# A two-layer trunk with streamed fp32 weights: second SwiGLUs that begin with a whole pair of blocks, and three smaller moves

## The chip, the cores and the metric

The kernel runs on one core of one Trainium2 chip. The metric is the device time of one launch in microseconds; lower is better. The names of the engines: PE is TensorE (matrix products), DVE is VectorE, ACT is ScalarE, POOL is GpSimd, SP is SyncE, which here issues the loads of weights. Each engine works off its own list of instructions in order and stops at the first one whose semaphore is not there yet.

## The reference

The input is 512 tokens of width 1024. Two layers, each of four stages, and a final RMSNorm:

```python
for i in range(DEPTH):                                     # DEPTH = 2
    h = h + 0.5 * swiglu(rmsnorm(h, ffn1_norm[i]), ffn1_w_gu[i], ffn1_w_down[i])
    u = rmsnorm(h, mix_norm[i])                            # the mixer: gated convolution + attention, 8 heads
    ...
    h = h + merged @ w_o[i]
    h = h + 0.5 * swiglu(rmsnorm(h, ffn2_norm[i]), ffn2_w_gu[i], ffn2_w_down[i])
    gate = jax.nn.sigmoid(rmsnorm(h, ple_norm[i]) @ w_ple_gate[i])
    h = h + gate * (p[i] @ w_ple_proj[i])
return rmsnorm(h, final_norm)

def swiglu(x, w_gu, w_down):
    g, u = jnp.split(x @ w_gu, 2, axis=-1)                 # D_FF = 2816 columns each
    return (jax.nn.silu(g) * u) @ w_down
```

All data are fp32, and the result has to be as good as fp32.

## The kernel before, in words

**Names.** The four stages of the layers 0 and 1 are called `a0`, `a1` (first SwiGLU), `m0`, `m1` (mixer), `b0`, `b1` (second SwiGLU), `e0`, `e1` (the gate with the per-layer input). Tiles begin with the stage's name: `b0x` is a normalised input of `b0`, `b00b` the PSUM tile "b" of quad 0 of `b0`, `a02d` the tile "d" of quad 2 of `a0`.

**Numbers.** A product in fp32 is three matmuls: an operand is split into a high part that PE takes at full rate and a low part (the rest), and `mm3` (lines 279 to 281) adds high·high, high·low and low·high. Activations lie with their 1024 features in 8 tiles of 128 partitions by 512 tokens (`h`), so a matmul of full width streams 512 columns.

**Weights.** SP loads them in pieces of 128 x 1024 (512 KB) into 10 buffers `st`. ACT makes the high part `wh` (line 71), DVE the rest `wl` (line 72), in 4 buffers each. Whatever PE does next thus has three things behind it: the load, ACT's cast and DVE's subtraction. Lines 150 to 168 (DVE) make sums and differences of weight pieces.

**A SwiGLU.** The 2816 columns of gate and up make 22 blocks of 128, in 11 pairs. A pair is done in one of two ways. *Whole*: 96 matmuls of 512 columns (8 tiles of features, gate and up of both blocks, three matmuls each). *By seven products*, a Strassen-Winograd scheme over blocks, halves of the features and halves of the tokens: the class `Quad` makes the combinations of weights, the class `Halved` those of the activations (`row(j)`: tiles `x`, `t`, `y`, `u`, lines 480 to 499 and their splits, once for each of four feature tiles), and `Sevens` has the steps. Its steps are numbered by product: 1, 2, 6 and 4 are *joint* ones (lines 545 and 549: 8 matmuls of 512 columns and 8 of 256), and 5, 7 and 3 are full ones (line 559: 24 of 256 columns) or joint, depending on the form. A step can begin with a *seed*: ACT copies a PSUM tile into another (line 565, 128 x 1024), and the next products are added to the copy. Each output goes through `finish` (lines 637 to 642: times 1/rms, Silu, gate times up). The down projection (`down`) runs beside later quads: a `pd` tile is seeded by ACT with twice the residual (line 680), the products are added to it, and ACT writes half of it back to `h` (line 684).

**What sets the order.** The program is written in the order in which PE is to work. Within that the framework's scheduler decides where ACT's and DVE's work stands in their lists; `tc.issue_after(x)` holds a piece behind an instruction.

**The normalisation.** `normed` makes the 8 inputs `x` of a stage from `h` without waiting for 1/rms; the sum of squares `acc` goes through a ones matmul (`ps`, lines 357 and 358), `rms` makes 1/rms (`r`, lines 361 to 365) from it, and `r` is multiplied in afterwards (`activate` for a whole block, lines 671 to 680, `finish` for the others).

**PSUM.** It has 8 banks of 128 x 512 fp32. `banks.paired()` shares them out as two double tiles "chain" (`PB`, banks 0 to 3), one double tile "seeded" (`PA`, banks 4 and 5) and two single ones (`PS`, banks 6 and 7). `banks.eight()` makes 8 single ones, for the attention and for the last stage `e1`.

**The four SwiGLUs differ in how they begin.** `a0` does its first 4 blocks (2 pairs) whole; `a1` its first 2 blocks (one pair), and two of the four `Halved` rows are made while the inputs come in. `b0` and `b1` do none whole: quads 0 and 1 are interleaved by hand, with special forms of `Quad` and `Sevens` ("early"), pieces of the token sums split one by one, and chains of `issue_after`.

**The mixer** ends its input projections with such quads too (`m1g3a`, `b`, `d`). Then come, for the first pair of heads, keys `kn0`, queries `qn0`, keys `kn1`, queries `qn1` and values `v0`, `v2`, each in a PSUM tile that must be split by ACT (line 271) and DVE (line 272) before the bank is used again.

Of the kernel before, what the change touches and what calls it, by code (L numbers as in the profile page):

```python
# [9 lines left out]
F32 = mybir.dt.float32  # L10
# [3 lines left out]
ALU = mybir.AluOpType  # L14
AX = mybir.AxisListType

P = 128
# [16 lines left out]
class Stream:  # L34
# [27 lines left out]
    def split(self, src, step=1024):  # L62
# [3 lines left out]
        for c in range(0, 1024, step):  # L66
            w = slice(c, c + step)
            if i == c == 0:
                self.nc.vector.tensor_copy(hi[:, w], src[:, w])
            else:  # L70
                self.nc.scalar.copy(hi[:, w], src[:, w])  # L71
            last = self.nc.vector.tensor_tensor(lo[:, w], src[:, w], hi[:, w].bitcast(F32), ALU.subtract)  # L72
        self.last_split = last.ins
# [57 lines left out]
class Quad:  # L131


    def __init__(self, W, quarters, early):
        self.W, self.early = W, early
        for q in ("a11", "a21", "a22", "a12"):
            setattr(self, q, W.raw(quarters[q]))

    def part(self, j):
# [12 lines left out]
        if self.early:  # L152
            if j == 5:
                self.s = W.buffer("s")
                tt(self.s, self.a21, self.a22, ALU.add)
                return W.split(self.s)
            if j == 6:
                tt(self.s, self.s, self.a11, ALU.subtract)  # L158
                return W.split(self.s)
            tt(self.a11, self.a11, self.a21, ALU.subtract)  # L160
            return W.split(self.a11)
# [32 lines left out]
def trunk_kernel(ctx, tc, dims, x, p, positions, gains, rope_c, final_row, weights, out):  # L194
# [263 lines left out]
    class Halved:  # L458
# [16 lines left out]
        def own(self, j, xs, parts=False):  # L475
# [7 lines left out]
            if parts:  # L483
                split_to(th[:, left], tl[:, left], t[:, left])
            self.ys[1].append(self.both(xs[j], left))
            self.ys[5].append((th[:, left], tl[:, left]))
            self.half[j] = x, t, th, tl, parts

        def other(self, j, xs):
# [4 lines left out]
            x, t, th, tl, parts = self.half.pop(j)  # L494
            y, u = G(f"{self.name}y{j}"), G(f"{self.name}u{j}")
            x_ins = nc.scalar.mul(y, h[k], gain(self.nm, self.l, k))
# [3 lines left out]
            at = right if parts else slice(0, S)  # L500
            split_to(th[:, at], tl[:, at], t[:, at])
# [3 lines left out]
            for p_, at in ((6, left), (4, right)):  # L505
                v = G(f"{self.name}u{j}_{p_}", F32R).rearrange("p (a t) -> p a t", t=H)
                last = split_to(v[:, 0, :], v[:, 1, :], u[:, at])
                self.ys[p_].append((v[:, 0, :], v))
            return x_ins.ins, last.ins

    class Sevens:
# [7 lines left out]
        def __init__(self, w, l, name, ys, columns, done, early=0):  # L519
            self.w, self.l, self.name, self.ys, self.columns, self.done, self.early = w, l, name, ys, columns, done, early  # L520
            self.todo = {}

        def quad(self, n):
            if n not in self.todo:
# [3 lines left out]
                self.todo[n] = {"w": Quad(W, quarters, n < self.early)}  # L528
            return self.todo[n]

        def split(self, n, j):

            d = self.quad(n)
            d["part", j] = d["w"].part(j)
# [4 lines left out]
        def joint(self, ps, d, j):  # L539

            hi, lo = d.pop(("part", j), None) or d["w"].part(j)
# [9 lines left out]
        def product(self, ps, d, j, start=False):  # L551

            hi, lo = d.pop(("part", j), None) or d["w"].part(j)
            for k, v in enumerate(self.ys[j]):
                vh, vl = v if j in (5, 7) else (v[0], v[1][:, 1, :])
                for w in range(2):
                    at = slice((2 * k + w) * P, (2 * k + w + 1) * P)
                    for i, (a_, b_) in enumerate(((hi, vh), (hi, vl), (lo, vh))):
                        nc.tensor.matmul(ps[:, w, :], a_[:, at], b_, start=start and w + k + i == 0,
                                         stop=k == 3 and i == 2, skip_group_check=True)  # L560
# [12 lines left out]
        def step(self, n, j):  # L573
            d, H, early = self.quad(n), self.H, n < self.early
            tt = nc.vector.tensor_tensor
            if j == 1:
                d["b"] = PB(f"{self.name}{n}b")
                self.joint(d["b"], d, j)
                if not early:
                    self.seed(n, "a")  # L580
            elif j == 2:
                self.joint(d["a"], d, j)
                self.out(n, d.pop("a"), 0, 0)
                if n + 1 < self.early:
                    self.seed(n + 1, "a")
            elif j == 6:
                self.joint(d["b"], d, j)
                if early:
                    d["u"] = [self.tile(n, f"u{w}") for w in range(2)]
                    for w in range(2):  # L590
                        nc.scalar.copy(d["u"][w], d["b"][:, :, w * H:(w + 1) * H])
                    tt(d["c5"], d["c5"], d["u"][1], ALU.add)
                else:
                    self.seed(n, "d")
            elif j == 5:
                d["c5"] = self.tile(n, "c5")
                if early:
                    d["c"] = PS(f"{self.name}{n}c").rearrange("p (w t) -> p w t", t=H)
                    self.product(d["c"], d, j, True)
                    nc.scalar.copy(d["c5"], d["c"])  # L600
                else:
                    self.product(d["d"][:, :, H:], d, j)
                    nc.scalar.copy(d["c5"], d["d"][:, :, H:])
            elif j == 7:
                self.product(d["b"][:, :, :H], d, j)
                t = d.pop("c5")
                tt(t, d["b"][:, :, :H], t, ALU.add)
                self.done(n, 1, 1, t, t)
            elif j == 3 and early:
                self.product(d["c"], d, j)  # L610
                t, l = d.pop("u")
                tt(t, t, l, ALU.add)
                tt(t, d.pop("c"), t, ALU.add)
                self.done(n, 0, 1, t, t)
# [7 lines left out]
    def ffn(l, nm, name, first=False, beside=iter(()), early=2):  # L622
# [6 lines left out]
        n_whole = 4 if first else 0 if early > 2 else 2  # L629
# [3 lines left out]
        def finish(n, f, c, src, t):  # L633
# [9 lines left out]
            if whole:  # L643
# [3 lines left out]
                        finish, 0 if n_whole else 2)  # L647
        step = sevens.step

        def early_rows(k, xs):  # L650

            j = k - KD // 2
            if n_whole == 0:
                if j < 0:
                    ys.own(k, xs, True)
                elif j < early:
                    ys.other(j, xs)
# [679 lines left out]
```

## Time and profile before

| | us |
|---|---|
| median of 3 runs (2284.45 to 2286.79) | 2286.35 |
| the profiled execution | 2286.7 |
| its span, first to last instruction | 2284.9 |
| PE busy | 2254.5 (99%), 12272 matmuls |
| DVE busy | 1746.8 (76%) |
| ACT busy | 1447.3 (63%) |
| DMA queue of the weights | 28.6% of 16 engines |

The span begins with the first instruction and ends with the last; 1.8 us of the profiled execution lie around it. A matmul's row gives its own duration (389 ns for 512 columns), but they are pipelined: the next one starts some 0.23 us after it. What a stretch of PE costs is therefore read from starts. PE is idle for 30 us in all, and the time is this idle time, what the clock gate takes, and the matmuls' own pace.

### The profile page before, as it was taken

The page shows a single profiled execution, that of the slowest core. Times are in us where ns is not written, and L with a number is a line of the kernel's source. Part 1 is how long each engine was busy: PE and PEld are TensorE (multiplying, and loading weights), DVE is VectorE, ACT ScalarE, POOL GpSimd, SP SyncE. Part 2 cuts the span into 40 slices and gives each one's busy share as a digit, 9 for nine tenths or more (in the row PEclk, how much of TensorE's full clock was granted, in tenths as well). Part 3 has the DMA queues.
Part 4 walks back from the last instruction along what each step waited for, and adds up shares of the span by engine and source line. Part 5 has one row for each costly group of instructions (what it writes and reads, how often), then busy time and mean ns, then how long its engine had stood idle before and what let it go on. Part 6 is the DMA issues. An engine that isn't in the chain of part 4 may idle for free.

```text
span 2284.9 us, 31443 instructions
## 1 busy us (share of the span) xinstructions
PE 2254.5 (99%) x12272; PEld 1959.8 (86%) x12272; DVE 1746.8 (76%) x2465; ACT 1447.3 (63%) x2250; POOL 40.4 (2%) x42
## 2 busy tenths in 40 slices
PE   9899999999999999999999999999999999999998
PEld 7788888888888888888888888888888888888887
DVE  7787766887877987776797777668878679777756
ACT  6666666456654666666676666655567466666664
POOL 0000000000210000000000000000002000000000
PEclk9999999999999999999999999999999999999999
DMA  5233232133121233324223333332221213332321
GB/s 213 87 103 105 99 132 99 65 102 102 47 93 65 84 120 102 111 96 146 83 78 107 102 102 111 111 102 83 93 74 65 102 37 125 107 111 101 111 94 37
DMA packets 63364, 223.07 MB, mean 98 GB/s; under 512 B 7280, under 2 KB 7280, under 8 KB 63216
## 3 DMA queue, kind: packets, MB, share of 16 engines
q1 hardware_dynamic: 62640, 220.28, 28.6%
q8 instruction: 96, 1.57, 0.3%
q10 hardware_dynamic: 576, 0.79, 0.1%
q14 instruction: 52, 0.43, 0.1%
HBM read 218.94 MB, written 2.10 MB: 97 GB/s over the span
## 4 chain that ended last, share of the span: by engine, by line
PE 93%; DVE 4%; ACT 2%; issue 0%; DMA 0%; SPq 0%; ACTq 0%; DVEq 0%
PE a1pd L279 2%; PE b1pd L279 2%; PE b0pd L279 2%; PE b1pd L280 2%; PE a1pd L280 2%; PE b0pd L280 2%; PE a0pd L279 2%; PE b0pd L281 2%; PE a1pd L281 2%; PE b1pd L281 2%; PE a0pd L280 2%; PE a0pd L281 2%; DVE wl L72 1%; ACT wh L71 1%; PE m0mop L279 1%; PE m1mop L279 1%
## 5 line engine op out<-in xcount | busy, mean ns | idle before, releaser
L72 DVE TENSOR_TENSOR wl<-st,wh 128x1024 fp32r<-128x1024 f32 (+1 forms) x504 | 610.6, 1213 | 320.4 <-ACT wh L71 318.7
L71 ACT CAST wh<-st 128x1024 fp32r<-128x1024 f32 (+1 forms) x503 | 523.4, 1044 | 414.7 <-PE b1pd L280 13.4
L72 DVE TENSOR_TENSOR wl<-s,wh 128x1024 fp32r<-128x1024 f32 x53 | 64.6, 1220 | 1.0 <-ACT wh L71 1.0
L71 ACT CAST wh<-s 128x1024 fp32r<-128x1024 f32 x53 | 55.1, 1040 | 12.8 <-DVE s L158 4.5
L150 DVE TENSOR_TENSOR st<-st,s 128x1024 f32<-128x1024 f32 x49 | 59.8, 1220 | 0.0
L163 DVE TENSOR_TENSOR st<-st,st 128x1024 f32<-128x1024 f32 x45 | 55.1, 1224 | 1.3
L165 DVE TENSOR_TENSOR s<-st,st 128x1024 f32<-128x1024 f32 x45 | 54.9, 1219 | 0.1
L168 DVE TENSOR_TENSOR st<-st,st 128x1024 f32<-128x1024 f32 x45 | 54.8, 1217 | 0.0
L684 ACT ACTIVATE h<-a0pd 128x512 f32<-128x512 f32 x41 | 24.3, 597 | 23.1 <-PE a0pd L281 23.0
L684 ACT ACTIVATE h<-b1pd 128x512 f32<-128x512 f32 x41 | 24.4, 597 | 21.6 <-PE b1pd L281 21.6
L684 ACT ACTIVATE h<-b0pd 128x512 f32<-128x512 f32 x41 | 24.4, 597 | 21.1 <-PE b0pd L281 21.0
L684 ACT ACTIVATE h<-a1pd 128x512 f32<-128x512 f32 x41 | 24.2, 597 | 19.0 <-PE a1pd L281 18.7
L680 ACT ACTIVATE b1pd<-h 128x512 f32<-128x512 f32 x41 | 24.6, 602 | 3.5 <-DVE b110o L570 1.4
L680 ACT ACTIVATE b0pd<-h 128x512 f32<-128x512 f32 x41 | 24.6, 602 | 3.5 <-DVE b010o L570 1.4
L680 ACT ACTIVATE a0pd<-h 128x512 f32<-128x512 f32 x41 | 24.5, 601 | 2.5 <-DVE a010o L570 1.7
L680 ACT ACTIVATE a1pd<-h 128x512 f32<-128x512 f32 x41 | 24.5, 601 | 2.2 <-DVE a110o L570 1.4
L108 POOL MEMSET wh<- 128x256 f32 x4 | 1.1, 312 | 1194.0 <-DVE wl L72 1194.0
L280 PE MATMUL a0p<-a0x,wh 128*128 128x512 f32 x44 | 17.2, 392 | 0.0
L281 PE MATMUL a0p<-a0x,wl 128*128 128x512 f32 x44 | 17.1, 389 | 0.0
L279 PE MATMUL a0p<-a0x,wh 128*128 128x512 f32 x44 | 17.1, 389 | 0.0
L274 ACT ACTIVATE b0x<-h,cols 128x512 fp32r<-128x512 f32 x8 | 5.8, 726 | 14.3 <-DVE h L1087 14.2
L274 ACT ACTIVATE b1x<-h,cols 128x512 fp32r<-128x512 f32 x8 | 5.8, 724 | 14.3 <-DVE h L1087 14.2
(6607 smaller groups left out, 7588.8 us busy)
## 6 DMA issues: line engine op xcount, KB each, us to landing
st<-in_weights SPq DMA_DIRECT2D x406, 512.0 KB, 3.3
h<-in_x SPq DMA_DIRECT2D x8, 256.0 KB, 5.4
st<-in_weights SPq DMA_DIRECT2D x7, 256.0 KB, 5.3
out<-e1d SPq DMA_DIRECT2D x4, 256.0 KB, 2.1
out<-fh SPq DMA_DIRECT2D x3, 256.0 KB, 2.2
e0pi<-in_p SPq DMA_DIRECT2D x2, 256.0 KB, 4.0
e1pi<-in_p SPq DMA_DIRECT2D x2, 256.0 KB, 3.8
fg<-in_final_row SPq DMA_DIRECT2D x2, 256.0 KB, 4.8
```

The source lines that it names most:

```text
L71: self.nc.scalar.copy(hi[:, w], src[:, w])
L72: last = self.nc.vector.tensor_tensor(lo[:, w], src[:, w], hi[:, w].bitcast(F32), ALU.subtract)
L150: tt(self.a12, self.a12, self.s, ALU.subtract)
L163: tt(self.a11, self.a11, self.a21, ALU.subtract)
L165: tt(self.s, self.a22, self.a11, ALU.subtract)
L168: tt(self.a21, self.a21, self.a22, ALU.add)
L274: nc.scalar.activation(hi, src, AF.Copy, scale=scale)
L279: nc.tensor.matmul(ps, wh, vh, start=first, stop=False, skip_group_check=seeded)
L280: nc.tensor.matmul(ps, wh, vl, start=False, stop=False, skip_group_check=seeded)
L281: nc.tensor.matmul(ps, wl, vh, start=False, stop=last, skip_group_check=seeded)
L680: nc.scalar.mul(ps, h[m], 2.0)
L684: nc.scalar.mul(h[m], ps, 0.5)
```

## The change

It has five parts.

1. **Second SwiGLUs (`b0`, `b1`).** They get the code of `a1`: the first pair of blocks is done whole, two of the `Halved` rows are made while the inputs come in, and the sevens begin with quad 1. All the code of the interleaved beginning is deleted. The keyword `early` now means the number of rows made ahead: 2 for `a1`, `b0`, `b1`, 0 for `a0`.
2. **The beginning of `a0`.** The rows 0 and 1 of the token sums come right behind the call that asks for 1/rms, row 2 behind the projections of block 2, and row 3 behind `activate(1)`. Before, all four came behind `activate(1)`.
3. **The mixer.** The first keys `kn0` go to a half of the PA tile and the first queries `qn0` to a half of a PB tile, so that `kn1`, `qn1` and `v0`, `v2` have the two single banks. The splits of the compressed queries and keys and of the rotary key stand behind step 2 of the last quad instead of behind step 6.
4. **The end of a SwiGLU.** The down projection's fourth remaining tile goes to half of a PB tile; it was the second half of the PA tile.
5. **The last stage `e1`.** Its first four projections of the per-layer input go to two PB tiles, and `banks.eight()` comes behind them. Before, `banks.eight()` came first.

The core of the diff (the deletion of the "early" forms in `Quad`, `Halved` and `Sevens` is cut):

```diff
-        n_whole = 4 if first else 0 if early > 2 else 2
+        n_whole = 4 if first else 2
...
         def early_rows(k, xs):
-            j = k - KD // 2
-            if n_whole == 0:
...
-            elif 0 <= j < early:
-                ys.row(j, xs)
+            if 0 <= k - KD // 2 < early:
+                ys.row(k - KD // 2, xs)
...
-        if n_whole == 0:
-            x_ins, sums = ys.other(KD // 2 - 1, xs)
-            with tc.issue_after(x_ins):
-                step(0, 1)
-                step(0, 5)
-            r = rms(acc, D, name, ps=halves(PA(name + "ps"))[0])
-            with tc.issue_after(x_ins):
-                step(1, 1)
-                step(1, 5)
-                sevens.seed(0, "a")
-            behind = sums
-            for n, j in ((0, 2), (0, 6), (0, 3), (0, 7), (1, 2), (0, 4), (1, 6), (1, 3), (1, 7)):
-                with tc.issue_after(behind):
-                    step(n, j)
-                behind = W.last_split
-            n0 = 1
...
+        if first:
+            pss[0], pss[1] = whole(0), whole(1)
+            projs(cs[0] + cs[1], xs, pss[0] + pss[1], True)
+            r = norm()
+            ys.row(0, xs)
+            ys.row(1, xs)
+            activate(0)
+            pss[2] = [PS(f"{name}p{w}2") for w in "gu"]
+            projs(cs[2], xs, pss[2])
+            ys.row(2, xs)
+            activate(1)
+            ys.row(3, xs)
+            pss[3] = whole(3)
+            projs(cs[3], xs, pss[3])
+            activate(2)
+            step(n0, 1)
+            activate(3)
...
+        else:
+            pss[0] = whole(0)
+            projs(cs[0], xs, pss[0])
+            r = norm()
+            for j in range(early, KD // 2):
+                ys.row(j, xs)
+            activate(0)
+            step(n0, 1)
+            pss[1] = [proj(cs[1][0], xs, f"{name}pg1")]
+            step(n0, 2)
+            step(n0, 6)
+            pss[1].append(proj(cs[1][1], xs, f"{name}pu1"))
+            step(n0, 5)
+            activate(1)
+            step(n0, 7)
+            step(n0, 3)
...
-        spare = halves(PA(f"{name}pd"))
+        spare = PA(f"{name}pd")[:, 0, :]
...
-                down(m, f0, nf, spare[1] if m == left[3] else None)
+                down(m, f0, nf, PB(f"{name}pb")[:, 0, :] if m == left[3] else None)
...
-                if (n_, j_) == (n_last, 6):
+                if (n_, j_) == (n_last, 2):
                     qc = [split(t, f"{name}qn{k}", paired=True) for k, t in enumerate(qt)]
                     kvc = [split(t, f"{name}kvn{k}") for k, t in enumerate(kvt)]
                     krh, krl = split(krt, name + "kr", paired=True)
...
-        pairs[0].keys_queries()
+        pairs[0].keys_queries(pss=(PA(name + "kn")[:, 0, :], PB(name + "qn")[:, 0, :]))
         banks.eight()
         pairs[0].values()
...
     def ple_last(l):
-        banks.eight()
...
-        ins = [inputs(0)]
+        ins = [inputs(0, sum((halves(PB(f"{name}pp0_{t}")) for t in range(0, NT, 2)), []))]
+        banks.eight()
...
-        ffn(l, "ffn2", f"b{l}", early=3)
+        ffn(l, "ffn2", f"b{l}")
```

How the instructions move is seen at three places. The changed file has other line numbers: its lines 268 to 270 are `mm3` (279 to 281 before), 525 and 529 a joint product (545 and 549), 260 and 261 a split (271 and 272), 543 the seed's copy (565), 620 and 622 Silu and product of `activate` (672 and 674).

PE where `b0` begins. Before, behind the last output projection of the mixer (`m0wop`), the joint product 1 of quad 0 and the full product 5 of quad 0, in tile `b00c`:

```order
L281 MATMUL m0wop_6768<-m0mg7h,wl_6784 128x512
L545 MATMUL b00b<-b0x_6800,wh_6923 128x512 x2
L545 MATMUL b00b<-b0x_6813,wh_6923 128x512 x2
L545 MATMUL b00b<-b0x_6827,wh_6923 128x512 x2
L545 MATMUL b00b<-b0x_6841,wh_6923 128x512 x2
L549 MATMUL b00b<-b0x_6800,wl_6924 128x256 x2
L549 MATMUL b00b<-b0x_6813,wl_6924 128x256 x2
L549 MATMUL b00b<-b0x_6827,wl_6924 128x256 x2
L549 MATMUL b00b<-b0x_6841,wl_6924 128x256 x2
L559 MATMUL b00c<-b0t0h,wh_6929 128x256
```

Now, the end of the whole pair's first block (tile `b0p`), the two ones matmuls, and quad 1 as the first one by seven products:

```order
L270 MATMUL b0p_6892<-b0x_6882,wl_6926 128x512
L346 MATMUL b0ps<-b0ah,ones 128x512
L347 MATMUL b0ps<-b0al,ones 128x512
L525 MATMUL b01b<-b0x_6801,wh_7023 128x512 x2
L525 MATMUL b01b<-b0x_6806,wh_7023 128x512 x2
L525 MATMUL b01b<-b0x_6812,wh_7023 128x512 x2
L525 MATMUL b01b<-b0x_6818,wh_7023 128x512 x2
L529 MATMUL b01b<-b0x_6801,wl_7024 128x256 x2
```

Quad 0 is gone from PE's list, 96 matmuls of `b0p`, `b0pg` and `b0pu` stand in its place, and quad 1 begins behind the ones matmuls.

ACT in `a0` around the seed of `a02a`. Before (`a0x`, `a0y`, `a0t`, `a0u` are the tiles of the token sums, `a0t2h` that of row 2):

```order
L565 COPY a02a<-a02b 128x1024
L496 ACTIVATE a0y_452<-h_95,cols 128x512
L271 CAST a0t2h<-a0t_447 128x512
L271 CAST a0u_6_460<-a0u_453 128x256
L271 CAST a0u_4_463<-a0u_453 128x256
L480 ACTIVATE a0x_466<-h_92,cols 128x512
L71 CAST wh_709<-st_559 128x1024
L496 ACTIVATE a0y_472<-h_96,cols 128x512
L271 CAST a0t3h<-a0t_467 128x512
L271 CAST a0u_6_480<-a0u_473 128x256
L271 CAST a0u_4_483<-a0u_473 128x256
L71 CAST wh_738<-st_557 128x1024
```

Now:

```order
L260 CAST a0a1h<-a0un_457 128x512
L469 ACTIVATE a0x_466<-h_92,cols 128x512
L71 CAST wh_664<-s 128x1024
L483 ACTIVATE a0y_472<-h_96,cols 128x512
L71 CAST wh_690<-st_688 128x1024
L260 CAST a0t3h<-a0t_467 128x512
L543 COPY a02a<-a02b 128x1024
L260 CAST a0u_6_480<-a0u_473 128x256
L260 CAST a0u_4_483<-a0u_473 128x256
L71 CAST wh_708<-st_559 128x1024
L620 ACTIVATE a0gn_547<-a0gn_547 128x512
```

Behind the seed's copy stood two rows of token sums, ten instructions with a weight cast among them; now two casts of the last row stand there.

DVE in `m1`, around the splits of keys and queries. Before (`m1h0qr` is the rotary part of the queries):

```order
L272 TENSOR_TENSOR m1h0kn0l<-m1h0kn_15424,m1h0kn0h 128x512
L862 TENSOR_TENSOR m1g3o_15413<-m1g3o_15413,m1r 128x512
L272 TENSOR_TENSOR m1h0qn0l<-m1h0qn_15441,m1h0qn0h 128x512
L72 TENSOR_TENSOR wl_15689<-st_15686,wh_15688 128x1024
L272 TENSOR_TENSOR m1h0kn1l<-m1h0kn_15455,m1h0kn1h 128x512
L924 TENSOR_TENSOR m1h0qr_15466<-m1h0qrt_15384,m1h0qr_15466 64x512
L924 TENSOR_TENSOR m1h0qr_15469<-m1h0qrt_15384,m1h0qr_15469 64x512
L272 TENSOR_TENSOR m1h0qn1l<-m1h0qn_15472,m1h0qn1h 128x512
```

Now:

```order
L261 TENSOR_TENSOR m1h0kn0l<-m1kn,m1h0kn0h 128x512
L797 TENSOR_TENSOR m1g3o_15321<-m1g3o_15321,m1r 128x512
L261 TENSOR_TENSOR m1h0qn0l<-m1qn,m1h0qn0h 128x512
L261 TENSOR_TENSOR m1h0kn1l<-m1h0kn_15363,m1h0kn1h 128x512
L72 TENSOR_TENSOR wl_15597<-st_15594,wh_15596 128x1024
L859 TENSOR_TENSOR m1h0qr_15374<-m1h0qrt_15292,m1h0qr_15374 64x512
L859 TENSOR_TENSOR m1h0qr_15377<-m1h0qrt_15292,m1h0qr_15377 64x512
L261 TENSOR_TENSOR m1h0qn1l<-m1h0qn_15380,m1h0qn1h 128x512
```

The weight's subtraction moved behind the split of `kn1`; the split of `qn1` stays last. In the changed program the tile of `v2` takes the bank of `qn1` in both layers; before, it took that of `kn1` in layer 0 and that of `qn1` in layer 1.

More of the change, by code (lines that the diff above doesn't have):

```diff
@@ L606, in step @@
                 t = d.pop("c5")
-                tt(t, d["b"][:, :, :H], t, ALU.add)
+                nc.vector.tensor_tensor(t, d["b"][:, :, :H], t, ALU.add)
                 self.done(n, 1, 1, t, t)
[L609 to L614, printed above, removed]
             elif j == 3:
```

162 lines of the change are left out of this document (47 added, 115 removed).

## The prediction

> **What bounds the kernel now.** I read the page first: PE is busy for 2254.5 of 2284.9 us and makes up 93% of the chain that ended last, so every gap of PE counts in full, and a gap elsewhere counts only if PE waits for it. Then the table of waits, PE alone (us in total, times, longest):
>
> ```profile
> PE a02a L545 <- ACT a02a L565: 2.4, 1, 2.4
> PE a02b L545 <- DVE a0u L272: 2.2, 1, 2.2
> PE a02d L559 <- ACT a02d L565: 2.0, 1, 2.0
> PE a0pd L279 <- ACT a0pd L680: 1.3, 1, 1.3
> ...
> PE b01b L545 <- ACT wh L71: 1.0, 1, 1.0
> ...
> PE e1pp L1149 <- ACT h L684: 0.7, 1, 0.7
> ```
>
> Nearly all of these waits stand at the four places that the change touches: the beginning of `a0` (8 us), the first heads of both mixers, the first quads of `b0` and `b1`, the first products of `e1`. There is no wait of `a1` among them.
>
> The third view is the granted clock in narrow windows (us, PE busy and instructions, clock, DMA share and GB/s):
>
> ```profile
> 52.46:55.87 3.41, 1.04 (x7) 1.00 0.48 154
> 55.87:59.29 3.42, 3.42 (x11) 0.50 0.00 0
> ...
> 72.94:76.35 3.41, 1.42 (x9) 1.00 0.00 0
> 76.35:79.77 3.42, 3.42 (x9) 0.50 0.24 66
> 779.50:782.91 3.41, 1.68 (x11) 1.00 0.43 131
> 782.91:786.33 3.42, 3.40 (x16) 0.50 0.63 195
> ...
> 1909.31:1912.72 3.41, 3.41 (x18) 0.50 0.78 255
> ```
>
> Four times a stretch of 3.4 us runs at half speed, each right behind a stretch in which PE was busy for less than half of the time (1.0 to 1.7 us of 3.4). Each takes 3.42 x 0.5 = 1.7 us beyond the waits themselves. [...]
>
> **Second SwiGLUs.** `b0` and `b1` get the program of `a1`, matmul for matmul. So I take their price from the stretch of `a1`, from its first matmul to the first of the mixer, against the stretches from the first matmul of `b0` and `b1` to the first of the next stage (columns: us, busy of PE, weight load, DVE, ACT, POOL, clock, DMA share, GB/s):
>
> ```profile
> 1145.51:1485.26 339.75, 339.75 (x1907) 297.76 (x1906) 259.48 (x323) 228.91 (x337) 0.00 (x0) 1.00 0.31 103
> 745.88:1090.62 344.74, 340.94 (x1956) 300.46 (x1954) 266.97 (x329) 231.85 (x341) 0.00 (x0) 1.00 0.33 110
> 1871.64:2216.37 344.73, 340.95 (x1956) 300.45 (x1954) 264.57 (x324) 228.97 (x335) 0.00 (x0) 1.00 0.32 107
> ```
>
> 344.74 - 339.75 = 5.0 us each, 10.0 for both. This is a balance, for PE gets *more* work. The rows for it are one third of the 48 matmuls of the first whole block of `a1` (first and last start), and in `b0` a full product followed by a joint one:
>
> ```profile
> L279 PE MATMUL a1p<-a1x,wh x16: 389/389/389, 1145.5 to 1155.7; 128*128 128x512 f32 x16
> ```
>
> ```profile
> 767.81 0.39 PE L559 MATMUL b00b<-b0t0h,wh 128*128 128x256 f32 x1 [0.30 <-ACT b00u L591]
> ...
> 770.84 2.00 PE L545 MATMUL b01a<-b0x,wh 128*128 128x512 f32 x8
> ...
> 773.64 2.00 PE L545 MATMUL b00b<-b0u,wh 128*128 128x512 f32 x8
> ```
>
> A matmul of 512 columns comes every 10.2 / 45 = 0.227 us, so a whole pair is 96 x 0.227 = 21.8 us. By seven products it is four joint ones of 2.8 and three full ones of 2.9 (3.03 less 0.16 of a slow start behind the gap), 19.9 us. That is 1.9 us more, against 6.9 that vanish: 344.74 - 340.94 = 3.8 of idle time, 1.7 of half clock (782.91, and 1909.31 in `b1`), and the rest slow starts behind the gaps. Bounds: if every loss goes, these 5.0; if they all come back in another form, a loss of 1.9.
>
> Does what stands ahead of `b0` let it run like `a1`? `a1` follows the gate stage, `b0` the output projection. The rows are the inputs' last step on DVE (count, duration, first and last start) and the low part of the sum of squares:
>
> ```profile
> L275 DVE SCALAR_TENSOR_TENSOR a1x<-h,cols,a1x x8: 743/746/751, 1118.4 to 1150.0; 128x512 fp32r<-128x512 f32 x8
> ...
> L275 DVE SCALAR_TENSOR_TENSOR b0x<-h,cols,b0x x8: 746/752/752, 709.5 to 747.7; 128x512 fp32r<-128x512 f32 x8
> ...
> L272 DVE TENSOR_TENSOR b0al<-b0acc,b0ah x1: 691/691/691, 749.8 to 749.8; 128x512 fp32r<-128x512 f32 x1
> ```
>
> The whole block takes the inputs one after the other, each for 6 matmuls, 1.36 us: the eighth at 745.88 + 9.5 = 755.4, the ones matmuls at 756.8. The eighth is ready at 748.4, the sum at 750.5. `a1` had its last input 5.2 us after its beginning, `b0` 2.5 us. So `b0` has more slack than `a1`, which waited for nothing. With a weight piece of 1024 columns feeding 24 matmuls (5.4 us) where a joint product takes 2.8, ACT's cast and DVE's subtraction (1.22 us, below) press less at the beginning. I take 5.0 each.
>
> **The beginning of `a0`.** PE's list stays as it is; what moves is ACT's and DVE's. PE before (start, duration, operation; in brackets the idle time ahead and its releaser):
>
> ```profile
> 51.84 1.11 PE L549 MATMUL a02b<-a0x,wl 128*128 128x256 f32 x8
> 55.33 3.36 PE L545 MATMUL a02a<-a0x,wh 128*128 128x512 f32 x8 [2.37 <-ACT a02a L565]
> ...
> 63.54 0.73 PE L545 MATMUL a02b<-a0u,wh 128*128 128x512 f32 x2 [2.19 <-DVE a0u L272]
> ...
> 66.48 0.50 PE L279 MATMUL a0pd<-a0a0h,wh 128*128 128x512 f32 x1 [1.25 <-ACT a0pd L680]
> ...
> 75.25 0.39 PE L559 MATMUL a02d<-a0t0h,wh 128*128 128x256 f32 x1 [1.99 <-ACT a02d L565]
> ```
>
> and ACT:
>
> ```profile
> 54.28 1.00 ACT L565 COPY a02a<-a02b 128x1024 f32<-128x1024 f32 x1
> ...
> 62.19 0.80 ACT L271 CAST a0u<-a0u 128x256 fp32r<-128x256 f32 x2
> ...
> 72.90 1.08 ACT L684 ACTIVATE h<-a0pd 128x512 f32<-128x512 f32 x2 [1.11 <-PE a0pd L281]
> ...
> 74.17 1.03 ACT L565 COPY a02d<-a02b 128x1024 f32<-128x1024 f32 x1
> ```
>
> Until 51.84 nothing should change for PE, if 1/rms and the blocks it scales stay in time. The seed's copy can begin when `a02b` is done, at 53.0; in ACT's new list it stands behind a cast of weights and one of row 3, and I put it at 53.6, so `a02a` begins at 54.6, 0.7 earlier. Behind it stand two casts (0.8 us) and DVE's two subtractions, about as long: the sums are ready near 56, where `a02a` (2.8 us) ends at 57.4; the 2.19 is gone. `a02b` ends at 60.2. The seeds of `a0pd` have by then had 4 us, so the 1.25 goes too. 24 matmuls of 0.227 us: the last starts at 65.4. In the trace the copy for `a02d` starts about 1.0 us after that matmul (the two writes to `h` are ahead of it) and takes 1.03: `a02d` at 67.5, against 75.25. That is 7.8 us, most of it waits, the rest the half clock at 55.87. Behind 67.5 PE does not fall below half of a window idle, so the second half-speed stretch (76.35) goes too: 1.7. Together 9.5. Bounds: all five gaps (8.3 with the 0.5 of another `a0pd`) and both half-speed stretches are 11.7; from below, 3.0, if rows 0 and 1 (some 3 us of each engine per row) push 1/rms and the blocks' activations back so far that the seeds of `a0pd` come late. The first gap, 53.0 to 54.6, lies in the window 52.46 to 55.87 and is 1.6 to 1.7 us: whether the clock falls behind it is open (1.7 us). I take that it does not, because the row with the smallest gap that did so has 3.41 - 1.68 = 1.73.
>
> **The mixer.** PE and DVE of layer 0, then PE of layer 1:
>
> ```profile
> 563.37 0.50 PE L279 MATMUL m0h0kn<-m0kvn0h,wh 128*128 128x512 f32 x1 [1.22 <-DVE m0h0kn0l L272]
> ...
> 568.34 0.28 PE L946 MATMUL m0h0v<-wh,m0kvn0h 128*128 128x256 f32 x1
> ```
>
> ```profile
> 564.43 1.22 DVE L72 TENSOR_TENSOR wl<-st,wh 128x1024 fp32r<-128x1024 f32 x1
> ...
> 567.42 1.41 DVE L924 TENSOR_TENSOR m0h0qr<-m0h0qrt,m0h0qr 64x512 fp32r<-64x512 f32 x2
> 568.86 0.69 DVE L272 TENSOR_TENSOR m0h0qn1l<-m0h0qn,m0h0qn1h 128x512 fp32r<-128x512 f32 x1
> ```
>
> ```profile
> 1687.77 0.50 PE L279 MATMUL m1h0kn<-m1kvn0h,wh 128*128 128x512 f32 x1 [1.19 <-DVE m1h0kn0l L272]
> ...
> 1693.99 0.39 PE L946 MATMUL m1h0v<-wh,m1kvn0h 128*128 128x256 f32 x1 [1.09 <-DVE m1h0qn1l L272]
> ```
>
> `kn1` no longer waits: 1.35 us at both places (1.22 and the slow start behind a gap). But `v2` now shares its bank with `qn1` in both layers. DVE's new list from 564.43 is the split of `kn1` (0.6), the weight (1.15), the rotary pair (1.4), the split of `qn1` (0.7): it ends at 568.3, and `v2` starts where it starts now, 568.34. The gain of `m0` is nothing: the wait moves from `kn1` to `v2`. In `m1`, 1124.4 us later by the starts of `kn1`, the same sum puts `v2` at 1692.8, against 1693.99: 1.2 gained. Bounds: 0 and 3.8 together (all three waits with their slow starts). The splits pulled ahead by some steps cost ACT and DVE nothing new, and PE has no wait there.
>
> **The last stage.** The 0.7 in the table is the bank 7 that `h`'s last write (line 684) must free; with its slow start PE loses 2217.94 - 2216.82 - 0.23 = 0.9:
>
> ```profile
> 2217.94 0.50 PE L1149 MATMUL e1pp<-wh,e1p0h 128*128 128x512 f32 x1 [0.73 <-ACT h L684]
> ```
>
> The PB tiles have long been free then: 0.9. The other tile for the end of a SwiGLU I put at nothing; PE does not wait there now, and if PB were late it would cost a write of `h`, 0.6 us, each.
>
> **Sum.** 10.0 + 9.5 + 1.2 + 0.9 = 21.6. The profiled execution is 2286.7 (span 2284.9 and 1.8 around it), 0.35 over the median; 2286.35 - 21.6 = 2264.8, so **2265 us**.
>
> **The rivals.**
> - *The moved rows only shift the waits of `a0`.* DVE and ACT work the same rows nearer to 1/rms, and the activations and seeds come later; `a0` gains 3 to 4. For it: rows 0 and 1 are 6 us of each engine around a chain that PE needs. Against: PE has whole blocks to do until 50 and waits for nothing there. 2286.35 - 10.0 - 3.5 - 2.1 = 2270.7. Chance 0.13.
> - *The second SwiGLUs keep half of their waits*, because DVE is behind when `b0` begins (it is busy for 39.10 of the 40 us from 760 to 800) and the new first pair only lends it 2 us of PE. Each gains 2: 2286.35 - 4.0 - 9.5 - 2.1 = 2270.7. Against it: the stretch of `a1`. With all losses kept and 1.9 more work each it is 2286.35 + 3.8 - 11.6 = 2278.6. Chance 0.12 for both.
> - *Hardly anything* (within 0.2%, 4.6 us, about what a measurement tells from no change): both of these in full. 0.02.
> - *Slower.* The whole pair takes the eight inputs in turn, and rows 0 and 1 now stand among them on ACT and DVE. If the scheduler lets them and weight casts go ahead of the last inputs, PE stands in the first block of `b0` and `b1`. The eighth input has 755.4 - 748.4 = 7 us of slack; two rows are 6 us, so it outweighs everything else only from delays of 16 us in each (7 of slack, 5 of gain, 5.8 for half of the other terms' 11.6, less 1.7 for a half-speed stretch behind such a gap). With 20 us it is 2286.35 - 11.6 + 2 x (20 - 7 - 5 + 1.7) = 2294. Chance 0.04.
>
> The likeliest has 0.69. Its own range goes from 2260 (mixer in full, `a0` at its bound) to 2269. For 8 in 10 I go up to the rivals at 2271 and somewhat beyond, to 2275, and down to 2259. Faster 0.93, the same 0.03, slower 0.04.
>
> **What would show it.** In the changed trace: the stretch from `b0`'s first matmul to `e0gp` at 339.8 and no wait of `b01b`; `a02d` at 67.5 and no half clock before 80; `kn1` without a wait and `v2` with one for `qn1`'s split in both layers; no wait in `e1pp`. I am wrong if a new wait of over 2 us stands in the first block of `b0`, or if 1/rms of `a0` comes more than 2 us later than in this trace.

## The result, and the profile after

The changed kernel takes 2266.28 us (median of 4 runs, 2265.78 to 2266.75) against 2286.34 us beside it (2284.45 to 2286.79): a ratio of 0.9914, with a 95% interval from 0.9897 to 0.9931. The profiled execution is 2266.17 us, its span 2264.0. The span is 20.9 us shorter; the forecast was 21.6. The medians differ by only 20.1: the profiled execution of the kernel before lay 0.35 over its median, and 2.2 us of a run lie around the span now, where it was 1.8.

The table of stages shows where they come from. First the changed kernel, from the first matmul of a stage to the first of the next, in the order `a0`, `m0`, `b0`, `a1`, `b1` (the rows of `e0` and `m1` are left to the text) and, last, `e1` to the end (columns: stretch, its length, busy time of PE, weight load, DVE, ACT and POOL, granted clock, DMA share, GB/s):

```profile
0.00:351.64 351.64, 347.46 (x1892) 301.64 (x1893) 275.51 (x364) 239.03 (x356) 0.68 (x6) 1.00 0.36 123
351.64:736.90 385.26, 383.05 (x2011) 331.05 (x2010) 294.78 (x482) 220.63 (x381) 19.87 (x18) 1.00 0.26 87
736.90:1076.64 339.74, 339.74 (x1908) 297.83 (x1906) 258.35 (x318) 227.91 (x334) 0.00 (x0) 1.00 0.33 107
1131.53:1471.27 339.74, 339.74 (x1907) 297.83 (x1906) 259.59 (x323) 228.76 (x337) 0.00 (x0) 1.00 0.31 103
...
1856.52:2196.28 339.76, 339.76 (x1908) 297.86 (x1907) 256.41 (x314) 224.99 (x329) 0.00 (x0) 1.00 0.31 104
2196.28:2264.00 67.72, 59.66 (x305) 50.33 (x303) 39.64 (x84) 36.48 (x57) 0.00 (x0) 0.98 0.09 32
```

The stretches of the kernel before that the prediction does not show, `a0`, `m0`, `m1` and the end, in the same view:

```profile
0.00:360.86 360.86, 351.51 (x1893) 303.71 (x1893) 276.00 (x364) 239.37 (x356) 0.68 (x6) 0.99 0.35 119
360.86:745.88 385.02, 383.16 (x2011) 330.82 (x2010) 299.42 (x494) 223.87 (x390) 19.86 (x18) 1.00 0.25 83
1485.26:1871.64 386.38, 383.45 (x2011) 330.87 (x2010) 299.34 (x494) 223.84 (x390) 19.87 (x18) 1.00 0.25 82
2216.37:2284.90 68.53, 59.86 (x305) 50.32 (x303) 39.64 (x84) 36.71 (x57) 0.00 (x0) 0.97 0.09 31
```

| stage | change measured | forecast |
|---|---|---|
| `a0` | -9.2 | -9.5 |
| `m0` | +0.2 | 0 |
| `b0` | -5.0 | -5.0 |
| `m1` (386.38 to 385.25) | -1.1 | -1.2 |
| `b1` | -5.0 | -5.0 |
| `e1` to the end | -0.8 | -0.9 |

`e0` and `a1` keep their 54.9 and 339.7 us. In `b0`, `a1` and `b1` PE is now busy for the whole stretch, with DVE at 76% and ACT at 67% of it beside (258.35 and 227.91 of 339.74 us in `b0`).

PE's four longest waits now, by the table of waits (us in total, times, longest):

```profile
PE a02a L525 <- ACT a02a L543: 1.7, 1, 1.7
PE m0h0v L881 <- DVE m0h0qn1l L261: 1.6, 1, 1.6
PE m1h0v L881 <- DVE m1h0qn1l L261: 1.6, 1, 1.6
PE a02d L538 <- ACT a02d L543: 1.2, 1, 1.2
```

The waits of `a02b`, `a0pd`, `b01b`, `e1pp` and of the keys `kn1` are gone. Two are left in `a0`, both for the copy that seeds a new tile, and each mixer has one that was not there before (`m0`) or was smaller (`m1`, 1.1): `v2` now waits for the split of `qn1`.

### The profile page after: what moved, and what is told of

It reads as the page before. It is cut to its first block, busy times and chain, and to the rows that moved or that the text cites. A ratio compares the mean times of both kernels' runs of the same rounds, so it can differ in the third digit from the quotient of the medians.

```text
span 2264.0 us, 31169 instructions
## 1 busy us (share of the span) xinstructions
PE 2247.3 (99%) x12176; PEld 1953.1 (86%) x12176; DVE 1721.0 (76%) x2423; ACT 1432.2 (63%) x2220; POOL 40.3 (2%) x42
## 4 chain that ended last, share of the span: by engine, by line
PE 98%; DVE 1%; ACT 1%; issue 0%; DMA 0%; SPq 0%; DVEq 0%; ACTq 0%
PE a1pd L268 2%; PE b1pd L268 2%; PE b0pd L268 2%; PE a0pd L268 2%; PE b1pd L269 2%; PE a1pd L269 2%; PE b0pd L269 2%; PE a1pd L270 2%; PE b0pd L270 2%; PE b1pd L270 2%; PE a0pd L269 2%; PE a0pd L270 2%; PE m0mop L268 1%; PE m1mop L269 1%; PE m0mop L269 1%; PE m1mop L270 1%
## 5 line engine op out<-in xcount | busy, mean ns | idle before, releaser
L152 DVE TENSOR_TENSOR st<-st,st 128x1024 f32<-128x1024 f32 x47 | 57.5, 1224 | 1.3
L72 DVE TENSOR_TENSOR wl<-s,wh 128x1024 fp32r<-128x1024 f32 x47 | 57.3, 1219 | 0.6 <-ACT wh L71 0.4
L157 DVE TENSOR_TENSOR st<-st,st 128x1024 f32<-128x1024 f32 x47 | 57.2, 1217 | 0.0
L71 ACT CAST wh<-s 128x1024 fp32r<-128x1024 f32 x47 | 49.0, 1042 | 8.8 <-PE a1p L269 2.6
```

Source lines behind the costliest of these rows:

```text
L157: tt(self.a21, self.a21, self.a22, ALU.add)
```

## The experiments

### Two parts, each by itself

The first run puts only the whole pair with its two rows into the kernel before; the second only the earlier token sums of `a0`.

```diff
 # second SwiGLUs alone, on the kernel before
-        ffn(l, "ffn2", f"b{l}", early=3)
+        ffn(l, "ffn2", f"b{l}", early=2)
 # (with the deletion of the interleaved beginning, as in the change)
```

> The kernel before with part 1 alone (second SwiGLUs begin with a whole pair). Theory: the gain lies within b0 and b1 and comes whole without the other parts: both stretches 339.8 us (before 344.7), no half clock near 780 and 1905, all other stages as before, so span 2284.9 - 9.9 = 2275.0 and time 2276.5. Rival (the stages depend on one another through weights loaded ahead and the scheduler, so that part of the gain needs the other parts): stretches between 341 and 345, time above 2279.

```diff
 # rows of a0 alone, on the kernel before
             r = rms(acc, D, name, ps=halves(PA(name + "ps"))[0])
             if first:
+                ys.row(0, xs)
+                ys.row(1, xs)
                 activate(0)
                 ...
                 projs(cs[2], xs, pss[2])
+                ys.row(2, xs)
                 activate(1)
-            for j in range(early, KD // 2):
-                ys.row(j, xs)
-            activate(n_whole - 2)
+                ys.row(3, xs)
                 ...
                 projs(cs[f], xs, pss[f])
+                activate(2)
                 step(n0, 1)
```

> The kernel before with part 2 alone (token sums of a0 moved up, the last activation behind block 3). Theory: a0 is shorter by 9.2 us as in the changed kernel, a02d begins at 67.6, granted clock 1.00 from 52 to 80; nothing else moves: span 2275.7, time 2277.1. Rival (a0's later stages catch up anyway, because the down projection's seeds or weights set the pace): the gain shrinks to under 6 by the end of a0, time above 2280.

The first took 2277.02 us (2276.94 to 2277.65), a ratio of 0.9959 (0.9945 to 0.9974) to the kernel before; the second 2277.7 (2277.18 to 2278.05), 0.9962 (0.9948 to 0.9976). The stretches of `b0` and `b1` in the first:

```profile
745.77:1085.52 339.75, 339.75 (x1908) 297.75 (x1906) 258.80 (x319) 227.92 (x335) 0.00 (x0) 1.00 0.31 107
1876.35:2216.10 339.75, 339.02 (x1903) 296.84 (x1902) 249.95 (x305) 226.11 (x333) 0.00 (x0) 1.00 0.30 103
```

Its `a0` stays at 360.73 us. The spans fall by 10.1 and by 9.0 us; both together are 19.1 of the 20.9. The 9.0 has to be read by stages, though. In the second run `a0` takes 352.30 us and not 351.64, because its first product by seven (`a02b`) starts at 50.79 us; this start moves from one profile to the next, also with the same kernel (50.12 and 50.70 in two profiles of the changed one). From there to the end of `a0` the second run gains 9.3 us on the kernel before, as the changed kernel does. The missing 0.7 is in part made up by 0.45 in `b0`, whose program is the old one; PE is busy there for 340.06 us, where it was 340.94. So each part gains alone what it gains with the other, 10.0 and 9.3, and the two large terms stand where the prediction put them. The rest is left for the mixer and the last stage, where the table above has 0.9 and 0.8. Parts 4 and 5 have no run of their own; for the last stage there is only the wait of `e1pp` that is gone.

### What makes the whole pair pay: the two rows made ahead

The prediction took the program of `a1` as one thing. This run takes one piece out: the same whole pair, with no `Halved` row made while the inputs come in.

```diff
-        ffn(l, "ffn2", f"b{l}")
+        ffn(l, "ffn2", f"b{l}", early=0)
```

> The changed kernel with none of the four rows of token sums of b0 and b1 made while the inputs come in (two in the changed kernel). Theory (the whole pair gives DVE 20 us before product 6 needs all rows, and the work until there is 4 rows of 3.1, 5 weight pieces of 1.2 and 4 combinations of 1.2, 23 us): PE waits 1 to 3 us at product 6, stretches 341 to 343 against 339.75, span 2266.5 to 2270.5. Rival (the whole pair alone gives slack enough, the rows ahead are worth nothing): 339.8, span 2264.

2281.86 us, 15.6 more than the changed kernel. The largest waits of `b0` and `b1`, the stretches of `b0` and `b1`, and the clock in two windows behind each other in `b0`:

```profile
PE b12b L525 <- ACT wh L71: 2.6, 1, 2.6
PE b02b L525 <- ACT wh L71: 2.6, 1, 2.6
...
PE b12d L538 <- ACT b12d L543: 1.1, 1, 1.1
PE b02d L538 <- ACT b02d L543: 1.1, 1, 1.1
```

```profile
737.48:1085.59 348.11, 342.66 (x1907) 298.77 (x1906) 264.09 (x331) 233.15 (x344) 0.00 (x0) 1.00 0.30 105
1865.47:2212.46 346.99, 341.09 (x1907) 297.52 (x1906) 261.90 (x327) 230.23 (x339) 0.00 (x0) 1.00 0.29 102
...
768.15:771.56 3.41, 0.81 (x4) 0.58 (x4) 2.45 (x3) 3.40 (x5) 0.00 (x0) 1.00 0.39 148
771.56:774.98 3.42, 3.42 (x12) 2.84 (x11) 3.42 (x5) 1.09 (x2) 0.00 (x0) 0.50 0.03 13
```

Without the two rows `b0` takes 8.4 us more and `b1` 7.2, and both take longer than in the kernel before (344.7). The whole pair alone is a loss of 2.3 to 3.4 us per layer. I had expected 341 to 343 us for each, which would still have been a gain. PE's timeline in `b0` shows the way of the delay:

```profile
759.85 1.09 PE L525 MATMUL b01b<-b0u,wh 128*128 128x512 f32 x4
...
766.25 0.62 PE L525 MATMUL b01b<-b0u,wh 128*128 128x512 f32 x2
...
770.88 3.25 PE L525 MATMUL b02b<-b0x,wh 128*128 128x512 f32 x8 [2.60 <-ACT wh L71]
```

ACT's casts of the fourth row end at 765.3 us; in the changed kernel they end at 754.7. So product 6 of quad 1 comes in pieces, with other matmuls between them, and ends late. ACT's next cast of a weight waits 1.64 us for it and starts at 766.90; a table load (1.28 us) and a Silu stand between it and the second cast (769.80 to 770.83), for which `b02b` waits. I had expected the wait at product 6 itself. The gain of `b0` and `b1` belongs to the two rows as much as to the pair.

### How far forward the rows of `a0` can go

Rows 0 and 1 went ahead of `activate(0)`. This run puts all four there.

```diff
             r = norm()
-            ys.row(0, xs)
-            ys.row(1, xs)
+            for j in range(4):
+                ys.row(j, xs)
             activate(0)
```

> The changed kernel with all four rows of token sums of a0 right behind the request for 1/rms. Theory (only two rows fit there): rows 2 and 3 (some 6 us of ACT and DVE) come ahead of the first block's activation, which ends near 43 instead of 37; block 3 needs its banks at 39.2, so PE waits 3 to 4 us there, and the clock may fall (1.7); the seed of a02a comes 0.5 earlier. a0 354 to 357 against 351.6, span 2266.5 to 2269. Rival (the earlier the rows the better, since PE has whole blocks to do until 50): no new wait, a0 351.0, span 2263.5.

2272.15 us, 5.9 more. The wait that came, PE's row of it, and the clock behind it:

```profile
PE a0p L268 <- ACT a0gn L620: 7.6, 1, 7.6
```

```profile
47.33 0.77 PE L268 MATMUL a0p<-a0x,wh 128*128 128x512 f32 x1 [7.64 <-ACT a0gn L620]
```

```profile
40.49:43.90 3.41, 0.00 (x0) 0.00 (x0) 3.41 (x5) 1.07 (x3) 0.00 (x0) 1.00 0.00 0
43.90:50.73 6.83, 3.40 (x8) 2.76 (x9) 5.94 (x12) 3.56 (x5) 0.00 (x0) 0.50 0.23 77
```

The Silu of the first block (`a0gn`) starts at 46.6 us instead of 35.2, and block 3 waits for its tile. This is the first rival's mechanism: it does not come with two rows there, and it does with four; three were not tried. Two rows, 6 us, fit in what PE has to do there; four do not. My estimate of the wait, 3 to 4 us, was half of what it was.

Two further runs moved row 3 alone, on top of the version with the later rotary parts (below), whose time is 2264.2. In one it stands ahead of `activate(1)`:

```diff
             ys.row(2, xs)
-            activate(1)
             ys.row(3, xs)
+            activate(1)
```

> The kernel with the rotary split last (span 2261.9), and in a0 row 3 moved the other way, ahead of the activation of block 1. Theory (there is room for about one row more than the changed kernel puts there): the cast of row 3 no longer stands ahead of the seed, a02a comes 0.5 earlier, but block 1's product comes 3 us later, near 49.7, where a02b needs its bank at 50.1: a wait of 0 to 1. a0 351.2 to 352.2. Rival (as with all four rows first, PE waits some us for the activation, with a half-speed stretch): a0 354 or more.

2265.68 us; `a0` takes 353.45 instead of 351.77, more than I had put at most (352.2). The seed's wait falls from 1.7 to 1.1, but a longer one for a Silu comes, and the clock falls behind it:

```profile
52.52 3.03 PE L525 MATMUL a02b<-a0x,wh 128*128 128x512 f32 x8 [2.36 <-ACT a0gn L620]
```

```profile
49.97:53.38 3.41, 1.05 (x5) 0.75 (x5) 3.41 (x6) 1.95 (x3) 0.00 (x0) 1.00 0.00 0
53.38:56.79 3.41, 3.41 (x13) 2.95 (x12) 2.62 (x5) 1.66 (x2) 0.00 (x0) 0.50 0.46 154
```

In the other it stands behind product 1 of quad 2, which then reads only three of the four rows: the kernel leaves out the fourth row's quarter of that product.

```diff
             activate(1)
-            ys.row(3, xs)
             ...
             step(n0, 1)
+            ys.row(3, xs)
```

> The kernel with the rotary split last (span 2261.9), and in a0 row 3 of the token sums moved behind the first product of quad 2. ACT's list then has two seeds of the down projection and the seed of a02a ahead of row 3, and PE's list has seven matmuls of a0pd between a02b and a02a. Theory (the 1.66 us gap is there because PE has nothing to do while ACT copies the seed, and the row stands ahead of it): the gap before a02a shrinks to under 0.3 and a02d comes 1.0 to 1.7 earlier, a0 350.2 against 351.7; span 2260.5. Rival (row 3 then comes too late for product 6, which needs all four): a wait of 1 to 2 us at a02b or a02d takes its place, a0 351.5 to 353.

2265.01 us, 0.8 more although it has less to compute. PE's two longest waits:

```profile
PE a0pd L268 <- ACT a0a3h L260: 2.8, 1, 2.8
PE a02d L538 <- ACT a02d L543: 1.9, 1, 1.9
```

The seed's wait is gone, as I had expected, but the fourth block's down products now wait for its activation (`a0a3h`), and `a02d` waits longer; the rival had the size right and named only the second of these waits. The place that the change chose for row 3 was the best of the three.

### The half clock behind the first gap of `a0`

The prediction left one thing open: whether the gap of 1.6 to 1.7 us ahead of `a02a` would bring the clock down. In the changed kernel it did not (3.41 us around the gap, and the next 3.41 us):

```profile
52.53:55.94 3.41, 1.75 (x10) 1.35 (x9) 3.32 (x7) 2.77 (x5) 0.00 (x0) 1.00 0.47 154
55.94:59.35 3.41, 3.41 (x19) 2.75 (x19) 2.68 (x5) 2.41 (x4) 0.00 (x0) 1.00 0.00 0
```

This run makes the gap longer: the seed takes 0.3 us more, by copying 128 of its 1024 columns a second time:

```diff
             nc.scalar.copy(d[what]..., d["b"]...)
+            if self.name == "a0" and n == 2 and what == "a":
+                nc.scalar.copy(d[what]...[:, :128], d["b"]...[:, :128])
```

> The changed kernel with one more copy of 128x128 on ACT behind the seed of a02a (the same data once more), so that PE's gap there grows from 1.66 us to about 1.9. [...]

```profile
52.56:55.97 3.41, 1.47 (x7) 1.08 (x7) 3.34 (x7) 2.72 (x6) 0.00 (x0) 1.00 0.42 154
55.97:59.38 3.41, 3.41 (x13) 3.03 (x12) 1.14 (x3) 1.85 (x3) 0.00 (x0) 0.50 0.00 0
```

```profile
54.74 2.76 PE L525 MATMUL a02a<-a0x,wh 128*128 128x512 f32 x8 [1.94 <-ACT a02a L545]
...
68.87 0.38 PE L538 MATMUL a02d<-a0t0h,wh 128*128 128x256 f32 x1 [1.14 <-ACT a02d L543]
```

0.28 us more of gap (1.94 against 1.66), which ends at nearly the same place (2.18 us into the 3.41 in both), and the clock behind it is 0.50 where it was 1.00. From the start of `a02b` to that of `a02d` it is 19.00 us against 17.53: 1.47 more, of which 0.28 is the gap and 1.2 the half clock. My estimate was 1.9 in all, 0.25 for the gap and 1.7 for the half-speed stretch; some 0.5 of the 1.7 was not paid.

### The mixer: which bank `v2` gets

First the paired banks alone are undone, with the rest of the change kept.

```diff
-        pairs[0].keys_queries(pss=(PA(name + "kn")[:, 0, :], PB(name + "qn")[:, 0, :]))
+        pairs[0].keys_queries()
```

> The changed kernel with the first keys and queries of the mixers back on the two single banks; the early splits stay. Theory (the banks decide): kn1 waits 1.2 us for kn0's split in both mixers, and behind it v2 waits about 1.1 for qn1's split, also in layer 0, where v2 now has qn1's bank. Both mixers 386.4 us, so m0 is 1.2 and m1 1.2 longer than in the changed kernel (385.2): span 2266.4. Rival (v2's wait for qn1's split alone sets the time, and a wait of kn1 ahead of it is hidden): both mixers 385.2, span 2264.

2268.07 us, `m0` and `m1` 386.39 each. The pair of waits, for `kn1` and for `v2`, that only `m1` had before now stands in both; this is PE in `m0`:

```profile
553.88 0.50 PE L268 MATMUL m0h0kn<-m0kvn0h,wh 128*128 128x512 f32 x1 [1.19 <-DVE m0h0kn0l L261]
...
560.11 0.39 PE L881 MATMUL m0h0v<-wh,m0kvn0h 128*128 128x256 f32 x1 [1.10 <-DVE m0h0qn1l L261]
```

So the banks are worth 1.1 us in each mixer of the changed kernel. With the early splits undone (back behind step 6 of the last quad) the mixers keep their 385.25:

```diff
-                if (n_, j_) == (n_last, 2):
+                if (n_, j_) == (n_last, 6):
```

> The changed kernel with the splits of the compressed queries and keys back behind step 6 of the last quad; the first keys and queries stay on the paired banks. Theory (the banks do all of part 3, the early splits only fill idle time): both mixers 385.2, span 2264.0. Rival (the early splits are what lets the first keys begin in time): a wait at the rotary queries or kn0 of 1 us or more in each mixer, span 2266 or more.

2266.59 us: no change in the mixers, as the prediction had it. What `v2` waits for in the changed kernel is DVE's list (start, duration, operation):

```profile
555.83 1.22 DVE L72 TENSOR_TENSOR wl<-st,wh 128x1024 fp32r<-128x1024 f32 x1
557.08 1.40 DVE L859 TENSOR_TENSOR m0h0qr<-m0h0qrt,m0h0qr 64x512 fp32r<-64x512 f32 x2
558.51 0.69 DVE L261 TENSOR_TENSOR m0h0qn1l<-m0h0qn,m0h0qn1h 128x512 fp32r<-128x512 f32 x1
```

The rotary pair, 1.4 us, stands ahead of the split on which `v2` depends, and nobody needs it so soon. The last experiment moves it behind the query:

```diff
             for t in range(2):
                 self.key(t, None if t else pss[0])
+                first = pss[0] is not None
                 if t:
-                    self.q_parts()
+                    if not first:
+                        self.q_parts()
                     ...
                 self.query(t, None if t else pss[1])
+                if t and first:
+                    self.q_parts()
```

> The changed kernel with the split of the rotary part of the first queries (q_parts) behind the projection qn1 instead of ahead of it, first pair of heads only. Theory (v2 waits for qn1's split because the weight and the rotary pair, 1.4 us, stand ahead of it on DVE): v2's wait falls from 1.57 us to about 0.3 in both mixers, each 1.3 shorter (383.9 against 385.25): span 2261.4. Rival (the split of qn1 is late because its cast on ACT is late; a table load now stands ahead of it): v2 waits as before, 385.2, span 2264.

2264.2 us; the mixers take 384.23 each, 1.0 less, where I had expected 1.3. The wait and its cause:

```profile
558.36 0.38 PE L881 MATMUL m0h0v<-wh,m0kvn0h 128*128 128x256 f32 x1 [0.55 <-DVE m0h0qn1l L261]
```

```profile
557.62 0.69 DVE L261 TENSOR_TENSOR m0h0qn1l<-m0h0qn,m0h0qn1h 128x512 fp32r<-128x512 f32 x1 [0.46 <-ACT m0h0qn1h L260]
```

DVE now waits for ACT: a table load of 1.28 us (at 555.61) stands ahead of ACT's half of the split, and keeps the last 0.5 us. To see whether this is a gain beyond the scatter, both kernels were timed in five rounds on one chip:

> The changed kernel itself once more, on the chip of the next run: 2266.3 us as before, span 2264.0 give or take 0.5.

> The changed kernel with the rotary split last, timed beside it. Theory (each mixer 1.02 us shorter, as its one look showed): 2264.2 us, 2.0 to 2.1 below the changed kernel, every run of it below every run of the other. Rival (the look was a lucky position of the clock's windows): no difference beyond 0.5 us.

The changed kernel took 2266.57 us (2265.93 to 2266.73), a ratio of 0.9915 (0.990 to 0.993); the one with the rotary parts last 2264.33 (2264.06 to 2264.66), 0.9906 (0.9889 to 0.9922). Every one of its runs lies below every run of the other: 2.2 us for one call moved, and the best of the versions.

## Why the prediction was right

- **What bounds the kernel.** That PE's list sets the time held: `b0` and `b1` have no gap of PE left, and they now take what `a1` takes, 339.74 us. Whether every gap counts in full was not tested gap by gap, and a half-speed stretch behind a gap counted for less than its 1.7 in places, see below.
- **Second SwiGLUs, 5.0 each.** Measured 5.0 and 5.0, in the change and alone. The step that carried it was to take the balance from a whole stretch of the same program, not from the sum of its parts. That the eight inputs come in time held too: no wait stands in the first block. What the prediction did not see is that the two rows made ahead decide the sign: its rival *slower* counts them as a danger. They were part of the stretch that it measured by, so the number was right without the reason; the run without them is its correction.
- **The beginning of `a0`, 9.5.** Measured 9.2, or 9.3 from the start of `a02b`. `a02a` was put at 54.6 and `a02d` at 67.5; they start at 54.71 and 67.65. From `a02d` to the end of the stage it was 285.6 us and is 284.0: 1.6 for the second half-speed stretch, put at 1.7. The step "PE's list stays as it is" was wrong: some of block 2's and block 0's down products now stand between the matmuls of `a02b`. This view is PE's timeline, where the first of them cuts product 6 in two:

```profile
57.62 1.55 PE L525 MATMUL a02b<-a0u,wh 128*128 128x512 f32 x6
59.06 0.50 PE L268 MATMUL a0pd<-a0a0h,wh 128*128 128x512 f32 x1
...
63.46 0.62 PE L525 MATMUL a02b<-a0u,wh 128*128 128x512 f32 x2
```

 The scheduler uses the freed time for whatever is ready. It cost nothing here: the same matmuls lie between the same two ends, and the copy for `a02d` starts right behind the two writes to `h`, as the prediction had it. That the clock did not fall behind the first gap (1.00 from 55.94 to 59.35) was luck in part: with a gap 0.28 us longer it was 0.50 there, and where the half-speed stretches begin differs from profile to profile (last section). That it would stay full behind `a02d` rested on an edge at half of a window, which no run shows; measured is a clock of 1.00 there and up to 2260.94 us, behind PE's last matmul.
- **The mixers, 0 and 1.2.** Measured +0.2 and -1.1. "The wait moves from `kn1` to `v2`" is what the trace shows. `v2`'s wait of 1.57 is 0.35 over the one of `kn1` that it replaces, so the 0 of `m0` was a small loss. `v2` was put where it stood: 568.34 less the 9.2 that `a0` and the start gained is 559.1; it starts at 559.26.
- **The last stage, 0.9.** 0.8; `e1pp` waits no more. The other tile at the end of a SwiGLU was put at nothing, and no wait shows it.
- **The price of a half-speed stretch, 1.7.** This term was too large at most places: 1.6 behind `a02d`, 1.2 in the run with the longer seed, at most 1.1 between `b0` and `b1` of the run without rows (348.11 with one, 346.99 without). In the kernel with only the rows of `a0` moved, `b0` and `b1` run the same program (columns as above); from PE's busy time I take it that `b1` has a half-speed stretch, as in the kernel before (340.95 us, and 0.50 from 1909.31 on), and `b0` none:

```profile
737.33:1081.62 344.29, 340.06 (x1955) 299.03 (x1954) 266.72 (x329) 231.76 (x341) 0.00 (x0) 1.00 0.32 111
1862.65:2207.39 344.74, 340.99 (x1955) 300.47 (x1954) 264.49 (x324) 228.90 (x335) 0.00 (x0) 1.00 0.31 107
```

 0.45 us. PE's busy time is 0.93 longer, but its idle time 4.23 less 3.75 = 0.48 shorter: PE arrives 0.93 later at its waits, and they are shorter by half of that. By this estimate the stretch cost 0.45 of the 1.7. In the sum this hardly mattered: `b0` and `b1` were taken whole, and in `a0` the second stretch was worth 1.6.
- **The rivals.** *The moved rows only shift the waits* did not come with two rows and did with four. *Keep half of their waits* and *slower* did not come: no wait stands in `b0` and `b1`. Without the two rows waits do come, behind the first block.

## What to carry to other kernels

When an edit gives a stage the program of another stage, read its price from that stage's whole stretch and then ask which piece of it carries the gain, for one piece left out can turn the sign. Work that is moved ahead of a chain is free up to the slack that the waiting engine has there and costs in full beyond it, so count the slack in the same unit as the rows that move. When a wait is only handed to another instruction, look at the list of the engine that releases it: what stands ahead of the release without being needed is the next gain.

## What was not expected of the hardware

The half-speed stretches in these traces last 3.41 or 3.42 us, or twice that (6.83 with all four rows of `a0` first). In the kernel before, as long as PE has work, they begin at 55.87, 76.35, 782.91 and 1909.31 us, so 20.48, 706.56 and 1126.40 us lie between them: 6, 207 and 330 times 3.413. Counted back in steps of 3.41333 us (1853.44 / 543, all three together), the first step lies 1.3 us after the start of the span; the same count gives 1.4 us in the run with the longer seed (from 55.97), 2.2 with row 3 ahead (from 53.38), 2.9 with four rows first (from 43.90) and 0.1 without rows ahead (from 771.56). In the changed kernel the clock falls only at 2260.95 us, behind PE's last matmul; 646 steps ahead of that are 55.94, which is 1.3 too. So in these profiles the steps have no fixed place in the span, and by PE's busy time (340.94 and 340.06 us) one and the same `b0` had a half-speed stretch in the kernel before and none in the one with only the rows of `a0` moved.

In the 3.41 us ahead of a half-speed stretch PE was busy for 1.68 and 1.66 us (before, 779.50 and 1905.90), 1.47, 1.42, 1.05, 1.04, 0.81 or 0. Behind 1.75 us in the changed kernel the clock was 1.00. In `b1` of the run without rows ahead PE was busy for 1.72 us of the 3.41 from 1894.55 on, and the next eight matmuls of 512 columns, those of `b12b`, take 2.14 us; `b02b`'s eight took 3.25 at a clock of 0.50. But the busy time alone does not tell the two cases apart. These 3.40 us of the kernel before have 1.68 us as well, and the clock is 1.00 behind them, until 76.35:

```profile
62.70:66.10 3.40, 1.68 (x10) 1.00 0.33 124
```

What decides at 1.68 us is not shown by any run here. The prediction took half of 3.41 us, 1.71, as the edge for the end of `a0`; that was an estimate from its rows, and the row above does not bear it out.
